# Moving the final norm's weight multiplications of the early channels, and splitting the last scaling and its stores over two engines and two queues

## The chip, the cores and the metric

The kernel runs on one core of one Trainium2 chip. The metric is device microseconds (us) of one execution. A profiled execution comes with a trace in which time starts at the span's begin; TensorE is called PE there, the loading of its weights PEld, VectorE DVE, ScalarE ACT, GpSimd POOL and SyncE, which only issues DMAs here, SP.

## The reference

One layer of a decoder on 1024 tokens with 1024 channels, all float32. Only the end matters for this change:

```python
z = rms_norm(h, norm_ple_g[l])
gate = jax.nn.sigmoid(z @ w_ple_gate[l] + b_ple_gate[l])
h = h + gate * (p[l] @ w_ple_proj[l])
return rms_norm(h, norm_final_g)      # y = h * rsqrt(mean(h*h) + 1e-6) * norm_final_g
```

Ahead of it stand the input projection with a pooling mixer and a gated linear recurrence, the output projection, and a squared-ReLU MLP with 4096 hidden channels.

## The kernel before

All activations lie transposed, channels on the 128 partitions and tokens along the free dimension, until the last stage. The float32 products are made of float32r parts: a high and a low part of each operand, three matmuls for one (high by high, high by low, low by high). The MLP is multiplied by a scheme with seven block products in place of eight. TensorE is fed without a halt through most of the kernel.

The last stage is the gate (`ps_e`, from z and the gate weights), the projection of the per-layer input (`ps_j`), the residual sum and the final norm. The first 512 tokens are done with channels on partitions, for all eight channel blocks. For the other 512 tokens only channels 0 to 511, the *early* half, are done so. Their result is turned by DVE transposes within 32 by 32 blocks, a store to DRAM (`turn_out`, lines 1196 ff.) and a load (`turn_in`, line 1207), so that tokens come to lie on partitions. The *late* half, channels 512 to 1023, is computed with tokens on partitions from the start, in four blocks of 128 tokens, `i` = 0 to 3. `late[i]` is a tile of 128 tokens by 1024 channels; `quarter(i, 0)` is its early half of 512 channels, which comes from the turn, and `quarter(i, 1)` its late half.

For each block `i`:

- `gate_opened(i)`: the first of 24 gate matmuls, and DVE's addition of the bias to what it left in PSUM (line 1248). `gate_products` adds the other 23. The opening of block `i + 1` is put ahead of the last 12 products of block `i`, so the group that one sees in the trace is 24 matmuls, 11 of block `i`, 1 of `i + 1`, 12 of `i`.
- `token_proj(i)`: six matmuls of the projection (line 1263).
- `sigmoids(i)`: ACT's sigmoid of the gate (line 1278).
- `gated(i)`: DVE multiplies it by the projection (line 1283) and adds the late half of the residual (line 1285).
- `early_square(i)`: ACT squares the early half and sums it over its channels (line 1223), into `early_mean[i]`.
- `early_gain(i)`: DVE multiplies the early half by the final norm's weights (line 1227), and adds the constant EPS to `early_mean[i]` (line 1228).
- `mean(i)`: DVE squares and sums the late half on top of `early_mean[i]` (line 1217), into `means[i]`.
- `inverse(i)`: POOL raises it to the power -0.5 (line 1288).
- `scale_late(i)`: DVE multiplies the late half by that and by the norm's weights (line 1292).
- `scale_early(i)`: ACT multiplies the early half, which has its weights already, by it (line 1296).
- `leave_for(i)`: SP issues one store of 512 KB, for blocks 0 to 2 (line 1301).

The last block runs through `token_last` (from line 1303 on): sigmoid and gating in two cuts of 256 channels; the sum of squares of the first cut on ACT (line 1314) and of the second on DVE; the root on POOL; then the scaling of both halves, and two stores of 256 KB (line 1327).

The order of instructions on PE, DVE and ACT in this stage is the order in which the code issues them: `pin` keeps it. Only `inverse`, which is all that POOL does, and the last two stores stand outside it. `early(0)` does the squares and weight multiplications of blocks 0 and 1 while block 1 is at its gate, and `early(2)` those of blocks 2 and 3 right after the mean of block 1.

Of the kernel before, what the change touches and what calls it, by code (L numbers as in the profile page):

```python
# [40 lines left out]
NTOK = 4  # L41
NQUAD = 4 * P
# [21 lines left out]
def block_kernel(  # L64
# [17 lines left out]
    nc = tc.nc  # L82
# [23 lines left out]
    def leave(name):  # L106
        spaces.pop(name).close()
# [24 lines left out]
    def bank(name):  # L132
        return pd.tile([P, HALF], F32, tag="pd", name=name)
# [27 lines left out]
    def got(ps):  # L161
        if ps.shape[-1] > HALF:
            return ps.rearrange("p (b j a) -> p b a j", b=2, a=2)
        return ps.rearrange("p (j a) -> p a j", a=2)

    def by(x, ps):
        if ps.shape[-1] > HALF:
            return x.rearrange("p (b a j) -> p b a j", b=2, a=2)
        return x.rearrange("p (a j) -> p a j", a=2)
# [7 lines left out]
    def pin(ins):  # L177
        return tc.keep_in_program_order(ins) if in_order else ins
# [324 lines left out]
    for k in range(NT):  # L503
# [3 lines left out]
        for hs in halves:  # L507
            if k == hs.start == 0:
                whi, wlo = (t[:, :HALF] for t in weight_tiles("wl0"))
                g = col("g_mix", 0)  # L510
                x, zhi, zlo = (t[:, hs] for t in (H[0], *A[0]))
# [9 lines left out]
            x, zhi, zlo = (t[:, hs] for t in (H[k], *A[k]))  # L521
# [597 lines left out]
    early_mean, means, inverses = ([ms[:, 4 * x + i : 4 * x + i + 1] for i in range(NTOK)] for x in range(3))  # L1119
# [45 lines left out]
    token_out = out[:, NT * HALF :].rearrange("p (i x) -> p i x", i=NTOK)  # L1165
# [35 lines left out]
    def quarter(i, half):  # L1201
        return late[i][:, half * NQUAD : (half + 1) * NQUAD]
# [9 lines left out]
    def mean(i, cut=slice(0, NQUAD)):  # L1212

        n = cut.stop - cut.start
        x = quarter(i, 1).rearrange("p (g x) -> p g x", g=4)[:, :, cut.start // 4 : cut.stop // 4]
        pin(
            nc.vector.tensor_tensor_reduce(
                square[:, :n].rearrange("p (g x) -> p g x", g=4), x, x, 1.0 / D, early_mean[i], ALU.mult, ALU.add, means[i]
            )
        )  # L1220

    def early_square(i):
        pin(nc.scalar.activation(T[5][:, SECOND], quarter(i, 0), AF.Square, scale=D**-0.5, accum_out=early_mean[i]))

    def early_gain(i):
        x = quarter(i, 0)
        pin(nc.vector.tensor_tensor(x, x, g_row[:, :NQUAD], ALU.mult))
        pin(nc.vector.tensor_scalar_add(early_mean[i], early_mean[i], EPS))

    def token_slice(i):  # L1230
# [20 lines left out]
    def token_gate(i, pg):  # L1251
        gate_products(i, pg, range(1, 12))
        ahead = gate_opened(i + 1) if i < NTOK - 1 else None
        gate_products(i, pg, range(12, 3 * NT))
        return ahead

    def token_proj(i, pj, cut):
        ts = token_slice(i)
        for k, (hi, lo, wh, wl) in enumerate(ple):
            for n, (z, w) in enumerate(((hi, wh), (hi, wl), (lo, wh))):  # L1260
                w = w[:, NQUAD + cut.start : NQUAD + cut.stop]
                pin(
                    nc.tensor.matmul(
                        pj, z[:, ts], turns(w), start=k == n == 0, stop=k == len(ple) - 1 and n == 2
                    )
                )
# [7 lines left out]
    def sigmoids(i, pg, cut=slice(0, NQUAD)):  # L1274
        t = T[3 + i % 2][:, FIRST]
        whole = cut.stop - cut.start == NQUAD
        got_a, by_a = (got(pg), by(t, pg)) if whole else (got(pg)[:, cut.start // 256], t[:, cut])
        pin(nc.scalar.activation(by_a, got_a, AF.Sigmoid))

    def gated(i, pj, cut=slice(0, NQUAD)):  # L1280

        t, e = T[3 + i % 2][:, FIRST][:, cut], T[3 + i % 2][:, SECOND][:, cut]
        pin(nc.vector.tensor_tensor(by(e, pj), by(t, pj), got(pj), ALU.mult))
        y = quarter(i, 1).rearrange("p (g o x) -> p g o x", g=4, x=32)[:, :, cut.start // P : cut.stop // P]
        pin(nc.vector.tensor_tensor(y, y, e.rearrange("p (o g x) -> p g o x", g=4, x=32), ALU.add))

    def inverse(i):
        nc.gpsimd.tensor_tensor(inverses[i], means[i], power, ALU.pow)

    def scale_late(i, cut=slice(0, NQUAD)):  # L1290
        y = quarter(i, 1)[:, cut]
        pin(nc.vector.scalar_tensor_tensor(y, y, inverses[i], g_row[:, NQUAD:][:, cut], ALU.mult, ALU.mult))

    def scale_early(i, cut=slice(0, NQUAD)):
        x = quarter(i, 0)[:, cut]
        pin(nc.scalar.activation(x, x, AF.Identity, scale=inverses[i]))

    def leave_for(i, cut=slice(0, NQUAD)):
        to = token_out[:, i].rearrange("p (h x) -> p h x", h=2)
        tc.keep_in_program_order(  # L1300
            nc.sync.dma_start(to[:, :, cut], late[i].rearrange("p (h x) -> p h x", h=2)[:, :, cut])
        )

    def token_last(i, pg, pj):

        cuts = slice(0, 256), slice(256, NQUAD)
        for cut in cuts:
            sigmoids(i, pg, cut)
        scale_early(i - 1)
        leave_for(i - 1)  # L1310
        gated(i, pj[0], cuts[0])
        y = quarter(i, 1).rearrange("p (g x) -> p g x", g=4)[:, :, :64]
        pin(
            nc.scalar.activation(
                T[5][:, HALF : HALF + 256].rearrange("p (g x) -> p g x", g=4), y, AF.Square, scale=D**-0.5, accum_out=means[i - 1]
            )
        )
        gated(i, pj[1], cuts[1])
        pin(nc.vector.tensor_tensor(early_mean[i], early_mean[i], means[i - 1], ALU.add))
        mean(i, cuts[1])  # L1320
        inverse(i)
        scale_early(i, slice(0, 256))
        rest = quarter(i, 0)[:, 256:]
        pin(nc.vector.tensor_scalar_mul(rest, rest, inverses[i]))
        scale_late(i)
        for half in range(2):
            nc.sync.dma_start(token_out[:, i, half * NQUAD : (half + 1) * NQUAD], quarter(i, half))

    for g, hs in enumerate(GROUPS):
        if g == 1:  # L1330
# [2 lines left out]
        for n, o in enumerate(ORDER[g]):  # L1333
# [14 lines left out]
            if g == 0 and 1 <= n < 5:  # L1348
                raw = wp.tile([P, S], F32, tag="raw", name=f"wg0_{n + 3}_raw")
                nc.sync.dma_start(raw, w_gate[n + 3])  # L1350
                x = slice((n - 1) * P, n * P)
# [27 lines left out]
    def early(first):  # L1379

        for x in range(first, first + 2):
            early_square(x)
            early_gain(x)

    in_order[:] = [True]
    opened = gate_opened(0)
    for i in range(NTOK):
        end = i == NTOK - 1
        pg, pj = opened
        if end:  # L1390
            token_gate(i, pg)
            pj = [x[:, :256] for x in (pj, bank("ps_j_end"))]
            for a, x in enumerate(pj):
                token_proj(i, x, slice(256 * a, 256 * a + 256))
            token_last(i, pg, pj)
            continue
        token_proj(i, pj, slice(0, NQUAD))
        opened = token_gate(i, pg)
        if i == 1:
            early(0)  # L1400
            mean(0)
            inverse(0)
        sigmoids(i, pg)
        if i > 0:
            scale_late(i - 1)
            scale_early(i - 1)
            leave_for(i - 1)
        gated(i, pj)
        if i == 0:
            continue  # L1410
        mean(i)
        inverse(i)
        if i == 1:
            early(2)
        if i == 2:
            scale_late(i)
    in_order.clear()
    leave("late")
    leave("sums")
# [80 lines left out]
```

## Time and profile before

| what | value |
|---|---|
| median of 3 runs | 919.76 us (919.32 to 919.93) |
| the profiled execution | 919.68 us |
| its span | 917.9 us, 11247 instructions |
| granted TensorE clock, mean | 0.998 |
| PE busy | 907.8 us (99%) |
| DVE busy | 700.8 us (76%) |
| ACT busy | 466.3 us (51%) |
| POOL busy | 39.1 us (4%) |

The span runs from the first to the last instruction; what the execution takes beyond it lies around the program. A row of the order of time gives the start in us, the duration in us, the engine, the line, the operation, what is written and read, the count, and in brackets how long the engine had been idle and what ended that. Successive instructions of one engine can overlap a little, so the pitch from start to start is shorter than the duration. A row of waits gives who waited for whom, the sum in us, the number of waits and the longest. A row of a DMA line gives the us from issue to landing, least, median and most. "edge" holds the small columns of sums and roots, "t_h" scratch tiles, "late" the blocks of the last stage, "turn" the buffers in DRAM through which the early half is turned.

### The profile page before, as it was taken

How to read it: one execution, taken by the hardware profiler on the slowest of the kernel's cores; microseconds unless marked ns; L12 is line 12 of the kernel's file. 1: busy time of each engine (PE TensorE's matmuls, PEld its weight loads, DVE VectorE, ACT ScalarE, POOL GpSimd, SP SyncE). 2: the span in 40 equal slices, each digit the busy share in tenths (PEclk: the TensorE clock that was granted, in tenths of full speed). 3: DMA queues.
4: the chain of work that ended last, by engine and by line, in shares of the span. 5: the costliest groups of instructions: out<-in, count | busy, mean ns of one | idle time of the engine just before them, and what ended most of it. 6: DMA issues, size and time to landing. Idle time of an engine off the chain costs nothing.

```text
span 917.9 us, 11247 instructions
## 1 busy us (share of the span) xinstructions
PE 907.8 (99%) x4221; PEld 791.2 (86%) x4221; DVE 700.8 (76%) x872; ACT 466.3 (51%) x602; POOL 39.1 (4%) x62
## 2 busy tenths in 40 slices
PE   9999999999999999999999999999999999999996
PEld 7888888888888888888888888888888888888885
DVE  7999974668876567656756899899876679799665
ACT  6569892447554454445444654353343436555322
POOL 4300001000000000000000000000000000000001
PEclk9999999999999999999999999999999999999999
DMA  7211145214478667766864987466633341041363
GB/s 273 101 47 45 48 160 144 76 46 120 111 206 223 201 167 229 224 184 176 243 196 165 355 321 278 138 202 203 205 113 100 115 161 46 1 138 47 104 181 117
DMA packets 56871, 142.47 MB, mean 155 GB/s; under 512 B 4976, under 2 KB 9968, under 8 KB 56816
## 3 DMA queue, kind: packets, MB, share of 16 engines
q1 hardware_dynamic: 52992, 132.31, 43.5%
q0 software_dynamic: 2736, 8.91, 5.8%
q10 hardware_dynamic: 1088, 0.52, 0.3%
q8 instruction: 33, 0.54, 0.3%
q14 instruction: 22, 0.18, 0.1%
HBM read 106.08 MB, written 35.65 MB: 154 GB/s over the span
## 4 chain that ended last, share of the span: by engine, by line
PE 96%; DMA 1%; DVE 1%; issue 1%; SPq 0%; POOL 0%; ACT 0%; DVEq 0%; POOLq 0%; ACTq 0%
PE ps_P_d L363 32%; PE ps_b_u L363 12%; PE ps_i L363 9%; PE ps_o L363 9%; PE ps_d_u L363 8%; PE ps_a_u L363 8%; PE ps_e L363 8%; PE ps_l L363 3%; PE ps_P_u L363 3%; PE ps_l L557 1%; PE ps_j L363 1%; PE ps_g L626 1%; PE ps_l_second L363 1%; PE ps_p L363 1%; DMA turn<-late 0%
## 5 line engine op out<-in xcount | busy, mean ns | idle before, releaser
L363 PE MATMUL ps_P_d<-a,wd_P_hi 128*128 128x512 f32 x880 | 261.8, 379 | 0.0
L363 PEld LDWEIGHTS ps_P_d<-a,wd_P_hi 128*128 128x128 f32 x880 | 166.5, 189 | 23.5
L363 PE MATMUL ps_P_d<-a,wd_P_lo 128*128 128x512 f32 x440 | 166.9, 379 | 0.0
L363 PE MATMUL ps_b_u<-a,wu_P 128*128 128x512 f32 x504 | 113.6, 379 | 0.0
L363 PEld LDWEIGHTS ps_b_u<-a,wu_P 128*128 128x128 f32 x504 | 95.3, 189 | 13.4
L363 PEld LDWEIGHTS ps_P_d<-a,wd_P_lo 128*128 128x128 f32 x440 | 83.2, 189 | 11.7
L363 PE MATMUL ps_a_u<-y,wu_P 128*128 128x512 f32 x360 | 82.6, 379 | 0.0
L363 PEld LDWEIGHTS ps_a_u<-y,wu_P 128*128 128x128 f32 x360 | 68.1, 189 | 9.6
L807 DVE TENSOR_TENSOR t_h<-t_h,ps_P_d 128x512 f32<-128x512 f32 (+1 forms) x56 | 42.4, 758 | 37.0 <-PE ps_P_d L363 37.0
L186 DVE TENSOR_TENSOR a<-wd,a 128x1024 fp32r<-128x1024 f32 x56 | 67.0, 1218 | 0.9 <-ACT a L185 0.6
L363 PE MATMUL ps_i<-a,wi_hi 128*128 128x512 f32 x256 | 66.1, 381 | 0.0
L363 PE MATMUL ps_o<-y,wo_hi 128*128 128x512 f32 x256 | 65.7, 379 | 0.0
L185 ACT ACTIVATE a<-wd 128x1024 fp32r<-128x1024 f32 x56 | 57.9, 1049 | 7.0 <-PE ps_P_d L363 7.0
L363 PEld LDWEIGHTS ps_i<-a,wi_hi 128*128 128x128 f32 x256 | 48.1, 189 | 7.9 <-PE ps_g L626 0.3
L185 ACT ACTIVATE wd_P_hi<-wd 128x1024 fp32r<-128x1024 f32 x24 | 25.3, 1056 | 58.0 <-PE ps_P_d L363 57.9
L363 PEld LDWEIGHTS ps_o<-y,wo_hi 128*128 128x128 f32 x256 | 48.4, 189 | 6.8
L825 DVE SCALAR_TENSOR_TENSOR t_h<-t_h,rstd 128x2048 f32<-128x2048 f32 x16 | 36.6, 2291 | 19.3 <-ACT t_h L844 19.3
L186 DVE TENSOR_TENSOR wu_P<-wu_raw,wu_P 128x512 fp32r<-128x512 f32 x45 | 30.9, 687 | 24.1 <-ACT wu_P L185 23.9
L186 DVE TENSOR_TENSOR wu_P<-wu,wu_P 128x512 fp32r<-128x512 f32 x47 | 32.3, 687 | 21.7 <-ACT wu_P L185 21.6
L363 PE MATMUL ps_d_u<-y,wu_P 128*128 128x512 f32 x180 | 41.3, 379 | 0.0
L363 PE MATMUL ps_d_u<-a,wu_P 128*128 128x512 f32 x180 | 41.3, 379 | 0.0
L185 ACT ACTIVATE wu_P<-wu 128x512 fp32r<-128x512 f32 x47 | 29.4, 625 | 20.0 <-PE ps_b_u L363 14.0
(252 smaller groups left out, 1538.6 us busy)
## 6 DMA issues: line engine op xcount, KB each, us to landing
wd<-act SPq DMA_DIRECT2D x56, 512.0 KB, 5.4
act<-t_h SPq DMA_DIRECT2D x32, 512.0 KB, 6.1
wu<-in_w_up SPq DMA_DIRECT2D x16, 512.0 KB, 4.9
act<-wu SPq DMA_DIRECT2D x16, 512.0 KB, 6.0
wd<-in_w_down SPq DMA_DIRECT2D x16, 512.0 KB, 5.9
wu_raw<-in_w_up SPq DMA_DIRECT2D x15, 512.0 KB, 5.3
t_h<-in_xT SPq DMA_DIRECT2D x14, 512.0 KB, 4.6
wg_raw<-in_w_gate SPq DMA_DIRECT2D x10, 512.0 KB, 3.3
```

Source lines behind the costliest of these rows:

```text
L185: first = pin(nc.scalar.activation(hi, src, AF.Copy))
L186: lowest[:] = [pin((eng or nc.vector).tensor_tensor(lo, src, f32(hi), ALU.subtract)).ins]
L363: ins = nc.tensor.matmul(ps, w, turns(z[:, hs]), start=first and z is zhi and w is whi, stop=last and w is wlo, skip_group_check=more,)
L557: nc.tensor.matmul(ps, kblk(w, o), turns(z[:, hs]), start=k == n == 0, stop=False)
L626: nc.tensor.matmul(x, w[r, o * P : (o + 1) * P], turns(z[r, at : at + HALF]), start=n == 0, stop=n == 2)
L807: (eng or nc.vector).tensor_tensor(to, to if y is None else y, x, ALU.add)
L825: nc.vector.scalar_tensor_tensor(cc, cc, 0.0, twice(R), ALU.max, ALU.mult)
```

## The change

The weight multiplication is cut loose from the addition of EPS, which becomes a function of its own, `floor`. `early` now only squares. The multiplication of block 0 comes after the mean and the root of block 0, that of block 1 after the mean and the root of block 1, those of blocks 2 and 3 after the late scaling of block 2. The additions of EPS stand right ahead of the mean that needs them, that of block 3 after the multiplications of blocks 2 and 3. In the last block ACT scales the whole early half, where DVE had taken the second 256 of its 512 channels, and the two last stores are issued one by ACT and one by SP, where SP had issued both.

```diff
     def early_gain(i):
         x = quarter(i, 0)
         pin(nc.vector.tensor_tensor(x, x, g_row[:, :NQUAD], ALU.mult))
+
+    def floor(i):
         pin(nc.vector.tensor_scalar_add(early_mean[i], early_mean[i], EPS))
...
         mean(i, cuts[1])
         inverse(i)
-        scale_early(i, slice(0, 256))
-        rest = quarter(i, 0)[:, 256:]
-        pin(nc.vector.tensor_scalar_mul(rest, rest, inverses[i]))
+        scale_early(i)
         scale_late(i)
-        for half in range(2):
-            nc.sync.dma_start(token_out[:, i, half * NQUAD : (half + 1) * NQUAD], quarter(i, half))
+        for half, queue in enumerate((nc.scalar, nc.sync)):
+            queue.dma_start(token_out[:, i, half * NQUAD : (half + 1) * NQUAD], quarter(i, half))
...
         for x in range(first, first + 2):
             early_square(x)
-            early_gain(x)
...
         if i == 1:
             early(0)
+            floor(0)
             mean(0)
             inverse(0)
+            early_gain(0)
         sigmoids(i, pg)
         if i > 0:
             scale_late(i - 1)
...
         gated(i, pj)
         if i == 0:
             continue
+        floor(i)
         mean(i)
         inverse(i)
         if i == 1:
             early(2)
+            early_gain(1)
         if i == 2:
             scale_late(i)
+            for x in range(2, NTOK):
+                early_gain(x)
+            floor(i + 1)
```

## The prediction

> **What bounds the kernel now.** I read the page first, then the waits of the last 34 us, then every instruction from 890 us in order of time, and last the stores to the output by line.
>
> ```profile
> span 917.9 us, 11247 instructions
> PE 96%; DMA 1%; DVE 1%; issue 1%; SPq 0%; POOL 0%; ACT 0%; DVEq 0%; POOLq 0%; ACTq 0%
> PE ps_e L1239 <- DVE ps_e L1248: 1.1, 1, 1.1
> ```
>
> The first two rows are the page's: 96% of the chain that ended last is TensorE. So an edit off TensorE pays only where TensorE stands still or after its last product. The third row is from the waits after 884 us: TensorE stands still once, for 1.1 us, and it is DVE that it waits for: the addition of the bias (L1248) that opens the gate product of a token block. The order of time shows why that addition is late.
>
> ```profile
> 890.62 5.34 PE L1239 MATMUL ps_e<-a 128*128 128x512 f32 x24
> 893.42 0.70 DVE L1248 TENSOR_TENSOR ps_e<-ps_e,t_h 128x512 f32<-128x512 f32 x1 [1.84 <-PE ps_e L1239]
> 894.96 0.69 DVE L1227 TENSOR_TENSOR late<-late,t_h 128x512 f32<-128x512 f32 x1 [0.84 <-ACT t_h L1223]
> 895.80 1.46 PE L1263 MATMUL ps_j<-proj,proj 128*128 128x512 f32 x6
> 896.40 0.57 ACT L1278 ACTIVATE t_h<-ps_e 128x512 f32<-128x512 f32 x1
> 897.10 5.34 PE L1239 MATMUL ps_e<-a 128*128 128x512 f32 x24
> 897.20 0.74 DVE L1217 CUSTOM_DVE_ANT_0 t_h<-late,edge 128x512 f32<-128x512 f32 x1
> 898.64 0.75 DVE L1292 SCALAR_TENSOR_TENSOR late<-late,edge,t_h 128x512 f32<-128x512 f32 x1 [0.69 <-POOL edge L1288]
> 899.31 0.68 DVE L1283 TENSOR_TENSOR t_h<-t_h,ps_e 128x512 f32<-128x512 f32 x1
> 900.75 0.75 DVE L1217 CUSTOM_DVE_ANT_0 t_h<-late,edge 128x512 f32<-128x512 f32 x1
> 901.43 0.69 DVE L1227 TENSOR_TENSOR late<-late,t_h 128x512 f32<-128x512 f32 x1
> 901.59 0.94 POOL L1288 TENSOR_TENSOR edge<-edge,power 128x1 f32<-128x1 f32 x1 [2.98 <-DVE edge L1217]
> 902.10 0.68 DVE L1227 TENSOR_TENSOR late<-late,t_h 128x512 f32<-128x512 f32 x1
> 902.48 0.60 ACT L1278 ACTIVATE t_h<-ps_e 128x512 f32<-128x512 f32 x1 [1.75 <-PE ps_e L1239]
> 902.76 0.69 DVE L1248 TENSOR_TENSOR ps_e<-ps_e,t_h 128x512 f32<-128x512 f32 x1
> 902.97 0.71 ACT L1296 ACTIVATE late<-late,edge 128x512 f32<-128x512 f32 x1
> 903.51 5.23 PE L1239 MATMUL ps_e<-a 128*128 128x512 f32 x23 [1.06 <-DVE ps_e L1248]
> 904.02 0.68 DVE L1283 TENSOR_TENSOR t_h<-t_h,ps_j 128x512 f32<-128x512 f32 x1
> 906.88 0.75 DVE L1292 SCALAR_TENSOR_TENSOR late<-late,edge,t_h 128x512 f32<-128x512 f32 x1 [0.66 <-POOL edge L1288]
> 908.77 0.66 ACT L1278 ACTIVATE t_h<-ps_e 128x256 f32<-128x256 f32 x2 [5.09 <-PE ps_e L1239]
> 909.51 0.42 DVE L1283 TENSOR_TENSOR t_h<-t_h,ps_j 128x256 f32<-128x256 f32 x1 [1.88 <-ACT t_h L1278]
> ```
>
> L1227 is the multiplication by the norm's weights. Four of them run; the two at 901.43 and 902.10 belong to blocks 2 and 3 and stand right before the bias addition of block 3 at 902.76. That addition needs only the first product of its group, and on the earlier block it came 893.42 - 890.62 = 2.80 after the group's start; so here it could run from 897.10 + 2.80 = 899.90. It runs 2.86 us later, and TensorE, through with its group, waits until 903.51. Much later, before 909.51, DVE is idle for 1.88 us.
>
> The tail after the last product:
>
> ```profile
> 911.10 0.15 DVE L1319 TENSOR_TENSOR edge<-edge 128x1 f32<-128x1 f32 x1
> 911.29 0.48 DVE L1217 CUSTOM_DVE_ANT_1 t_h<-late,edge 128x256 f32<-128x256 f32 x1
> 911.86 0.55 POOL L1288 TENSOR_TENSOR edge<-edge,power 128x1 f32<-128x1 f32 x1 [5.01 <-DVE edge L1217]
> 912.44 0.51 ACT L1296 ACTIVATE late<-late,edge 128x256 f32<-128x256 f32 x1 [1.45 <-POOL edge L1288]
> 912.44 0.35 DVE L1324 TENSOR_SCALAR late<-late,edge 128x256 f32<-128x256 f32 x1 [0.66 <-POOL edge L1288]
> 912.71 0.75 DVE L1292 SCALAR_TENSOR_TENSOR late<-late,edge,t_h 128x512 f32<-128x512 f32 x1
> 912.98 0.84 SPq L1327 DMA_DIRECT2D out<-late  x2
> ```
>
> And the stores: of line 1327 (the last two, 256 KB each) and of line 1301 (512 KB each, one per earlier block), from issue to landing; then the core's last waits; then the instruction queue in the window from 915 us:
>
> ```profile
> DMA to landing us min/median/max: 2.1/2.7/3.3
> DMA to landing us min/median/max: 2.6/2.6/2.6
> L1492 SPq EVENT_SEMAPHORE  x4: 28/28/28, 916.8 to 917.0; - x4
> q14 instruction: 1, 0.01, 0.7%
> ```
>
> The two issues take 0.33 us each, so the second is issued at 912.98 + 0.84 - 0.33 = 913.49, just behind the DVE scaling (912.71 + 0.75 = 913.46). It lands 3.3 us later, at 916.8, where SP's wait ends; the close takes the remaining 1.1 us to 917.9. The first half took only 2.1 us, and a whole block of 512 KB 2.6. The second half's surplus coincides with one packet of instruction code that a DMA engine moved from 915 us on.
>
> **The sum is made against** the profiled execution: 919.68 us, of which 917.9 is span and 1.78 lies around it. It is 0.08 under the median of the runs, 919.76. A measurement of this kernel tells about 0.2% (1.84 us) from no change, so "faster" begins at 917.92.
>
> **Part 1: the multiplications move, and the addition of the constant is split off.** No instruction is added or removed; four multiplications (0.69 us each, 0.60 from start to start without the small addition behind it: 902.10 - 901.43 = 0.67, of which that is 0.07) and four small additions change places on DVE. The new order, walked through with the pitches of these rows:
>
> - Block 0, from 894.96, when ACT's square lets DVE go: the small addition, then the mean. The mean reads its result, and such a pair stands 911.29 - 911.10 = 0.19 apart: mean at 895.15 instead of 897.20. POOL starts 901.59 - 900.75 = 0.84 after a mean, takes 0.55, and DVE follows 0.03 later (911.86 + 0.55 to 912.44): the reciprocal root is there at 896.57. Beside it runs the multiplication of block 0, 901.43 - 900.75 = 0.68 after the mean's start, at 895.83 to 896.52, hidden under POOL's time.
> - Late scaling of block 0 at 896.57 (before: 898.64). Gating of block 1 at 896.57 + 0.67 = 897.24; its sigmoid ended at 896.40 + 0.57 = 896.97, in time. Mean of block 1 at 897.24 + 1.44 + 0.11 = 898.79 (1.44 from 899.31 to 900.75; 0.11 for the small addition in front, 0.07 to 0.12). Multiplication of block 1 at 899.47, through at 900.07.
> - Bias addition of block 3 at 900.07 instead of 902.76, over at 900.76. TensorE needs it after its group: 897.10 + 5.18 = 902.28 (5.18 is the pitch 890.62 to 895.80). The wait is gone with 1.5 us to spare.
>
> What TensorE gains: the last group starts at 902.28 instead of 903.51, 1.23. Measured at the sigmoid that waits for its end: a group of 24 without a halt reaches its sigmoid 902.48 - 897.10 = 5.38 after its start, one of 23 by one matmul (5.18 / 24 = 0.22) less, 5.16; so at 907.44 instead of 908.77. **Gain 1.33** (bounds 1.06, the recorded halt, to 1.33). I take 1.33, which stands at the reader of the result.
>
> What is late next: the multiplications of blocks 2 and 3 now lie behind block 2's late scaling, ahead of the gating of block 3. Gating of block 2 waits for its sigmoid, 902.48 + 0.60, so 903.11 (before 904.02, behind DVE's queue); mean at 903.11 + 1.44 + 0.06 = 904.61; POOL 905.45 to 906.00; late scaling 906.03; multiplications 906.70 and 907.30; last small addition 907.90; DVE free at 907.97. The gating of block 3 wants to start at 909.51 - 1.33 = 908.18. So they fit into what was idle, with 0.2 us of cover; if POOL takes 0.94 as at 901.59, DVE is free at 908.36 and the end comes 0.2 later. Cost 0, bounds 0 to 0.4. On ACT, the early scaling of block 2 needs its multiplication (over by 907.4) and comes only after the last sigmoids, 908.1. The stores of blocks 0 and 1 are issued up to 2 us earlier by SP, into queues with nothing urgent. Nothing else in the kernel changes order.
>
> **Part 2: the last scaling.** ACT takes the whole early half (0.71, row 902.97, in place of 0.51), DVE loses its quarter (0.35; 912.71 - 912.44 = 0.27 from start to start) and begins with the late half at once. With the root there at 912.44 - 1.33 = 911.11, ACT ends at 911.82, DVE at 911.86. **Gain 0.27** for the last half.
>
> **Part 3: the stores.** One on ACT's queue, one on SP's, both issued at about 911.88, against 913.49 for the later one before: 1.60 earlier, which is the two gains together. How long do they take? Nothing in this trace issues two such stores at once. The bounds: 2.6 (512 KB by one issue; no reason for less, since the bytes are the same) and 3.3 (the second half before). ACT's queue was used once, beside SP's, for transposed blocks:
>
> ```profile
> turn<-late SPq DMA_DIRECT2D x4, 128.0 KB, 3.5
> turn<-late ACTq DMA_DIRECT2D x4, 128.0 KB, 4.0
> L1196 ACTq DMA_DIRECT2D turn<-late x4: 401/743/1257, 885.9 to 888.2; - x4
> ```
>
> There ACT landed 0.5 later, and its shortest issue was 0.40 against 0.33. I take 2.8: the 2.6 of the same bytes, 0.1 for ACT's longer issue and 0.1 for two at once. It is nearest to that row, because both halves then stream together as one block does, and the packet of code came at 915 us, behind SP's first landing: two landings close together leave it little data to delay. Landing at 911.89 + 2.8 = 914.7 instead of 916.8. **Gain 0.5 more** (bounds 0.7 to 0, and a loss of 0.5 where ACT lands as late as with the transposed blocks).
>
> The Trainium skill, page "DMA: Bandwidth & Descriptors", section "Issuing engines are not separate DMA queues", says that transfers started by different engines run on the same 16 DMA engines and interleave, and that issuing from several saves only the sequencer's time. By that rule the second queue is worth no more than one issue, 0.33, and the halves should land together. The trace does not show such a pair; that SP was held by DVE and not by its own first issue (913.46 against 912.98 + 0.33) speaks for the rule.
>
> **Sum:** 1.33 + 0.27 + 0.5 = 2.1; 919.68 - 2.1 = 917.6.
>
> **The rivals.**
>
> *The pair lands as the second half did, 3.3 after its issue.* For it: it is the only row of a last store with another in flight, and code for the close must still be fetched. Against it: the first half took 2.1, three whole blocks 2.6. Then only the earlier start counts: 919.68 - 1.33 - 0.27 = 918.1; with ACT 0.5 later still, 918.6. That is within 0.2%. The page's rule above goes this way: a second queue brings no shorter transfer.
>
> *DVE is late at block 3.* The cover is 0.2 us; a slow POOL, or a longer pitch of the moved multiplications, puts them on the path: 917.8 to 918.2.
>
> *The wait stays.* If the bias addition is held by something else than the multiplications, for instance the root of block 0 that stands ahead of the scaling, TensorE still waits and parts 2 and 3 alone remain: 919.68 - 0.27 - 0 to 0.5 = 918.9 to 919.4. Against it: the chain in DVE's order has no other late wait, and 1.5 us to spare.
>
> *Slower, by ACT's queue.* The ACT half is the last landing. It decides from 2.1 + 2.8 = 4.9 us after its issue: then nothing is gained. The longest landing of the transposed blocks, both queues, was
>
> ```profile
> DMA to landing us min/median/max: 2.1/3.6/5.5
> ```
>
> With 5.5: 911.87 + 5.5 = 917.4, 0.6 behind the old end: 920.3. Slower by over 0.2% needs 6.9. Against it: that row is of eight transposing stores at once, whereas a plain store of the same 2 KB rows landed in 2.6 three times out of three.
>
> **How the numbers follow.** Forecast, own range 917.3 to 918.0: 0.50. Long landing, 918.0 to 918.6: 0.28. DVE late: 0.10. Wait stays: 0.07. ACT's queue: 0.05, most of it within 0.2% of before. "Faster" (below 917.92) is the forecast without its upper edge and part of the DVE case: 0.50. Slower 0.03, the same 0.47. Low end: 2.6 for the pair and 0.3 that I have not seen, 917.1; high end 918.9, which leaves the unremoved wait and the very late queue outside.
>
> **What would show it.** TensorE's last gate group with no wait on L1248 and starting near 902.3; two multiplications between 906.5 and 908.0 on DVE; the first scaled quarter's gating near 908.2 waiting for ACT or TensorE, not queued; both stores issued within 0.1 us near 911.9; SP's last wait ending near 914.7. Wrong if that wait ends past 915.5, if the gating of block 3 runs back to back behind a multiplication, or if TensorE halts elsewhere.

## The result, and the profile after

The changed kernel takes 918.2 us in the median (917.72 to 918.95, 20 runs) against 919.94 (919.32 to 920.97, 20 runs) before: 1.74 us less, ratio 0.9981 with a 95% interval of 0.9974 to 0.9988. The profiled execution took 918.18 us; its span is 916.0. The order of time of the last stage, in the lines that answer to those shown of before (in this fence and the next, lines from 1228 to 1319 have a number 2 higher than before):

```profile
895.27 0.15 DVE L1230 TENSOR_SCALAR edge<-edge 128x1 f32<-128x1 f32 x1 [0.94 <-ACT t_h L1223]
895.46 0.75 DVE L1217 CUSTOM_DVE_ANT_0 t_h<-late,edge 128x512 f32<-128x512 f32 x1
896.13 0.69 DVE L1227 TENSOR_TENSOR late<-late,t_h 128x512 f32<-128x512 f32 x1
897.29 0.75 DVE L1294 SCALAR_TENSOR_TENSOR late<-late,edge,t_h 128x512 f32<-128x512 f32 x1 [0.47 <-POOL edge L1290]
897.32 10.31 PE L1241 MATMUL ps_e<-a 128*128 128x512 f32 x47
900.14 0.69 DVE L1227 TENSOR_TENSOR late<-late,t_h 128x512 f32<-128x512 f32 x1
900.75 0.69 DVE L1250 TENSOR_TENSOR ps_e<-ps_e,t_h 128x512 f32<-128x512 f32 x1
906.26 0.75 DVE L1294 SCALAR_TENSOR_TENSOR late<-late,edge,t_h 128x512 f32<-128x512 f32 x1 [0.66 <-POOL edge L1290]
906.93 1.29 DVE L1227 TENSOR_TENSOR late<-late,t_h 128x512 f32<-128x512 f32 x2
907.66 0.66 ACT L1280 ACTIVATE t_h<-ps_e 128x256 f32<-128x256 f32 x2 [3.75 <-PE ps_e L1241]
908.14 0.15 DVE L1230 TENSOR_SCALAR edge<-edge 128x1 f32<-128x1 f32 x1
908.40 0.42 DVE L1285 TENSOR_TENSOR t_h<-t_h,ps_j 128x256 f32<-128x256 f32 x1
```

The gate products of blocks 2 and 3 now stand in one row of 47 matmuls without a halt (before: 24, a halt of 1.06, 23). The bias addition starts at 900.75, right behind the multiplication of block 1, and is over 1 us before TensorE needs it. The two multiplications of blocks 2 and 3 fill 906.93 to 908.2, and the gating of block 3 starts at 908.40, 0.74 after its sigmoid as before (909.51 - 908.77). This execution was 0.22 later than that of before by 890 us, so the sigmoid at 907.66 stands for a gain of 1.33 where the clock difference shows 1.11.

The tail, then the landings of the last two stores, SP's last wait, and SP's closing instructions:

```profile
911.34 0.72 ACT L1298 ACTIVATE late<-late,edge 128x512 f32<-128x512 f32 x1 [1.45 <-POOL edge L1290]
911.34 0.75 DVE L1294 SCALAR_TENSOR_TENSOR late<-late,edge,t_h 128x512 f32<-128x512 f32 x1 [0.66 <-POOL edge L1290]
912.09 0.40 ACTq L1327 DMA_DIRECT2D out<-late  x1
912.12 0.33 SPq L1327 DMA_DIRECT2D out<-late  x1
DMA to landing us min/median/max: 2.4/2.6/2.8
SPq L1498 <- DMA out<-late: 2.2, 1, 2.2
L1498 SPq EVENT_SEMAPHORE  x11: 17/28/28, 912.5 to 916.0; - x11
```

Issues, landing and close are where the prediction put them, counted from the sigmoid: the last landing comes 7.2 after it, forecast 914.7 - 907.44 = 7.3. What it did not have is in no row of the span: this execution takes 918.18 - 916.0 = 2.18 us around its span, that of before 1.78. Over all 20 runs the time around the span is 2.08 to 2.18, median 2.13; for the kernel before, in the 30 runs of the first comparison below, 1.73 to 1.85, median 1.78.

### The profile page after: what moved, and what is told of

Same layout as the page of the kernel before. It is cut to its first block, busy times and chain, and to the rows that moved or that the text cites. A ratio compares the mean times of both kernels' runs of the same rounds, so it can differ in the third digit from the quotient of the medians.

```text
span 916.0 us, 11244 instructions
## 1 busy us (share of the span) xinstructions
PE 908.1 (99%) x4221; PEld 791.0 (86%) x4221; DVE 700.9 (77%) x871; ACT 466.7 (51%) x602; POOL 39.8 (4%) x62
## 4 chain that ended last, share of the span: by engine, by line
PE 98%; issue 1%; DVE 0%; ACT 0%; POOLq 0%; POOL 0%
PE ps_P_d L363 32%; PE ps_b_u L363 12%; PE ps_i L363 9%; PE ps_o L363 9%; PE ps_a_u L363 8%; PE ps_d_u L363 8%; PE ps_e L363 8%; PE ps_l L363 3%; PE ps_P_u L363 3%; PE ps_e L1241 2%; PE ps_l L557 1%; PE ps_j L363 1%; PE ps_g L626 1%; PE ps_p L363 1%; PE ps_l_second L363 1%
```

## The experiments

Two measures are used. *Tail* is the time in the trace from the start of block 3's first sigmoid to the end of the last instruction; it is free of what happened earlier, and kernels with the same tail gave it within 0.02. *Around* is the time of a run less its span, as the median of the runs.

| kernel | us, median | around | tail | VectorE's instructions |
|---|---|---|---|---|
| before | 919.94 | 1.78 | 9.13 | 1218 |
| changed | 918.20 | 2.13 | 8.39 | 1213 |
| order_only | 917.63 | 1.80 | 8.06 | 1214 |
| tail_only | 919.47 | 1.79 | 8.61 | 1217 |
| both_on_sp | 918.40 | 2.13 | 8.27 | 1213 |
| one_store | 918.00 | 2.16 | 8.35 | 1213 |
| changed_plus_1 | 917.56 | 1.79 | 8.37 | 1214 |
| changed_plus_5 | 919.05 | 1.76 | 9.27 | 1218 |
| before_plus_20 | 918.64 | 1.78 | 8.05 | 1238 |
| two_moved | 917.87 | 1.77 | 8.07 | 1216 |
| order_two_queues | 917.28 | 1.81 | 8.12 | 1214 |

The last column counts all rows of VectorE in the trace, semaphore and drain instructions too. The four kernels from order_only to one_store ran on one chip, the next four from changed_plus_1 to two_moved on a second and order_two_queues on a third, beside the kernel before each time (919.88, 919.96 and 919.71 there). Across chips the ratios below are the fairer measure. Each tail is that of one trace.

### The parts one by one

**order_only**, the changed kernel with the old tail:

```diff
-        scale_early(i)
+        scale_early(i, slice(0, 256))
+        rest = quarter(i, 0)[:, 256:]
+        pin(nc.vector.tensor_scalar_mul(rest, rest, inverses[i]))
         scale_late(i)
-        for half, queue in enumerate((nc.scalar, nc.sync)):
-            queue.dma_start(...)
+        for half in range(2):
+            nc.sync.dma_start(...)
```

> The changed kernel with the last scaling and the last stores as they were before (ACT 256 channels, DVE 256, both stores on SP). Theory (the bias addition's wait is the larger part, and comes from the order alone): TensorE's last gate group runs with no wait on the bias addition, the sigmoid of block 3 about 1.3 us earlier than before, span 917.9 - 1.3 = 916.6 if the second store lands 3.3 us after its issue again, 916.1 if it lands in 2.3 to 2.8. Rival (the gain is the tail's, the order only moves work about): span within 0.4 of 917.9. On the time around the span (1.78 before, 2.08 to 2.18 in the runs of the changed kernel): if the store on ACT's queue costs it, 1.8 here; if the order does, 2.1.

917.63 us, ratio to before 0.9973 (0.9962 to 0.9983): in the median more than the whole change brings. Time around the span 1.80, so it is not the order that costs it. The landings of its two last stores:

```profile
912.33 0.84 SPq L1329 DMA_DIRECT2D out<-late  x2
DMA to landing us min/median/max: 2.1/2.1/2.2
```

The issues are as far apart as before, on the same queue, and the second store lands in 2.2, not 3.3.

**tail_only**, the kernel before with the new tail:

```diff
-        scale_early(i, slice(0, 256))
-        rest = quarter(i, 0)[:, 256:]
-        pin(nc.vector.tensor_scalar_mul(rest, rest, inverses[i]))
+        scale_early(i)
         scale_late(i)
-        for half in range(2):
-            nc.sync.dma_start(...)
+        for half, queue in enumerate((nc.scalar, nc.sync)):
+            queue.dma_start(...)
```

> The kernel before with only the last scaling (ACT all of the early half, DVE the late half at once) and the last stores (one on ACT, one on SP) changed. Theory: TensorE still waits about 1.06 us for the bias addition; both stores are issued 0.27 earlier than the later one before, near 913.2, and land in 2.8 instead of 3.3: span 917.9 - 0.27 - 0.5 = 917.1. Rival (two queues bring nothing but the earlier issue): 917.6. Time around the span: 2.1 if the store on ACT's queue costs it, 1.8 if not; with 2.1 the whole is worth about 0.4.

919.47 us, ratio 0.9993 (0.9984 to 1.0001), so not told from no change by time; around 1.79 although a store is on ACT's queue. The halt, the issues and the landings:

```profile
903.46 5.23 PE L1239 MATMUL ps_e<-a 128*128 128x512 f32 x23 [1.03 <-DVE ps_e L1248]
913.15 0.41 ACTq L1325 DMA_DIRECT2D out<-late  x1
913.18 0.33 SPq L1325 DMA_DIRECT2D out<-late  x1
DMA to landing us min/median/max: 2.5/2.6/2.8
```

TensorE's halt stays: it belongs to the order. The tail is 8.61, between order_only's 8.06 and before's 9.13; the span of this trace, 917.3, lies between theory and rival. About 0.2 of it is a gap in VectorE's closing instructions in this trace (0.47 from its last but one semaphore to its drain, 0.11 before).

**both_on_sp** and **one_store**, the changed kernel with other last stores:

```diff
-        for half, queue in enumerate((nc.scalar, nc.sync)):
+        for half, queue in enumerate((nc.sync, nc.sync)):
```

and, for one_store,

```diff
-        for half, queue in enumerate((nc.scalar, nc.sync)):
-            queue.dma_start(token_out[:, i, half * NQUAD : (half + 1) * NQUAD], quarter(i, half))
+        nc.sync.dma_start(token_out[:, i], late[i])
```

> The changed kernel with both last stores issued by SP, one after the other. Theory (the second store was late before because it was issued late and met a packet of code; the queue itself brings little): issues at 912.1 and 912.45, second landing 2.4 to 2.8 after its issue, span 916.0 to 916.4. Rival (a second store behind the first on one queue takes 3.3 whatever comes): landing 915.8, span 916.9. Time around the span: 1.8 if the store on ACT's queue costs 0.35 there, so that the whole comes out at about 918.0 or better; 2.1 if it does not.

> The changed kernel with the whole last block in one store of 512 KB on SP. Theory: issue at 912.1, landing 2.6 later as the three whole blocks before it, 914.7; span 915.8, 0.2 less than the changed kernel. If the store on ACT's queue costs 0.35 around the span, that goes too: 917.6 in all. Rival (two queues stream faster than one): span 916.2 or more.

918.40 and 918.00; both within noise of the changed kernel (ratios to before 0.9983 and 0.9980, against 0.9981). Neither brings the time around the span down: 2.13 and 2.16. So ACT's queue does not cost it. The landings, of both_on_sp and of one_store:

```profile
DMA to landing us min/median/max: 2.1/2.2/2.3
DMA to landing us min/median/max: 2.6/2.6/2.6
```

A second store behind a first on one queue lands in 2.3: the 3.3 was not the queue's. By the tail, 8.27 and 8.35 against 8.39, two queues bring nothing; one store gains 0.04 of it, not the 0.2 expected.

### The packet of code

After these four, the time around the span went with the length of VectorE's stream and with nothing else tried: 1213 instructions gave 2.13 to 2.16, 1214 and more 1.78 to 1.80. Code comes in packets of 8 KB on the instruction queue q14. In the kernel before, 10 of its 22 packets come while VectorE is within nine instructions, mostly within three, of number 62, 190, 318 and so on, 128 apart; the last such step is near 1214. In the kernel before that packet falls among the last store's data (915.4); in all kernels with 1214 to 1217 instructions it comes 0.3 to 1.4 us after the span's end, with 1213 instructions 1.6 after it. Three kernels move this packet and leave the order of all else as it is. The filler is a memset of an unused column of 128x1, put where VectorE is idle near 888 us:

```diff
         opened = token_gate(i, pg)
+        for _ in range(N if i == 0 else 0):      # N = 1, 5 on the changed kernel, 20 on before
+            pin(nc.vector.memset(spare, 0.0))
```

> The changed kernel with one more tiny instruction on VectorE (a memset of an unused column, while VectorE is idle near 888 us). So far the time around the span was 1.78 to 1.80 where VectorE's stream had 1214 instructions or more (before, order_only, tail_only) and 2.13 to 2.16 where it had 1213 (the changed kernel, both_on_sp, one_store). Theory (0.35 us outside the span hang on how far VectorE's stream reaches, since its last block of code is fetched as it passes a certain instruction): 1214 instructions, time around the span 1.80, span unchanged near 916.05, in all 917.85. Rival (the ACT or SP side, or the total order, sets it): time around the span 2.13, in all 918.2.

917.56 us (ratio 0.9974, 0.9964 to 0.9984), around 1.79, tail 8.37. One instruction of no use takes 0.35 off the time around the span, and nothing else changes.

> The changed kernel with five such instructions: 1218 on VectorE, as in the kernel before. Theory (the packet of code comes as VectorE passes that instruction, and whatever store is in flight then lands late): the packet falls inside the span, about 2 us after VectorE's last scaling, near 914; the stores land 0.3 to 1.0 later than 2.8; time around the span 1.78; span 916.3 to 917.0. Rival (the second store before landed late for another reason): landing 2.8, span 916.05.

919.05 us (0.9988, 0.9979 to 0.9997), around 1.76, tail 9.27. Here are the landings, and the instruction queue's packet in the window from 913.9 to 914.5:

```profile
DMA to landing us min/median/max: 3.4/3.5/3.6
q14 instruction: 1, 0.01, 3.2%
```

The packet is back among the stores' data, and both land 0.8 to 1.0 later than in the changed kernel. The packet itself took about 0.3 us (3.2% of 16 engines over 0.6 us); why it costs three times that is not shown.

> The kernel before with twenty such instructions, all in an idle stretch of VectorE: the same order and the same tail, only the packet of code comes earlier, near 907. Theory: TensorE's wait of 1.06 stays, the second of the last stores lands 2.2 after its issue instead of 3.3, span 918.1 - 1.1 = 917.0, in all 918.8, which would be 1.1 of the change's 1.7 without any part of the change. Rival (two stores on one queue are slow by themselves): landing 3.3, 919.9 in all.

918.64 us, ratio 0.9984 (0.9975 to 0.9993): 1.32 less than before on this chip, about three quarters of what the change brings, with none of its edits. The packet came even earlier than expected, at 901.5. Its halt and its last stores' landings:

```profile
902.91 5.23 PE L1240 MATMUL ps_e<-a 128*128 128x512 f32 x23 [0.84 <-DVE ps_e L1249]
DMA to landing us min/median/max: 2.1/2.1/2.2
```

TensorE still halts, 0.22 less than before; why less is not shown, and it makes up the part of the 1.32 that the tail does not. The second store lands in 2.2, as order_only's does, and the tail is 8.05 instead of 9.13. So the 3.3 us were the packet of code, 1.08 of tail.

### Two of the four, and the tail's own price

**two_moved**, the kernel before with only two multiplications moved (`floor` is split off as in the change):

```diff
             early_square(x)
-            early_gain(x)
+            if first == 0:
+                early_gain(x)
+                floor(x)
...
+        if i == 2:
+            floor(i)
         mean(i)
...
             scale_late(i)
+            for x in range(2, NTOK):
+                early_gain(x)
+            floor(i + 1)
```

> The kernel before with only the multiplications of blocks 2 and 3 moved behind block 2's late scaling; those of blocks 0 and 1 and the whole tail stay as before. Theory (TensorE waits because two multiplications stand right ahead of the bias addition): bias addition at 902.76 - 1.33 = 901.4, over before TensorE needs it at 902.3, no halt; the same 1.3 us at block 3's sigmoid as with all four moved, and the span of order_only, 915.8, as long as the packet of code falls outside the last stores. Rival (all four moves are needed): a halt of some tenths stays.

917.87 us (0.9977, 0.9968 to 0.9987). The gate products of blocks 2 and 3 stand in one row of 47 again, but it takes 10.52 us, where all four moves gave 10.31:

```profile
897.61 10.52 PE L1241 MATMUL ps_e<-a 128*128 128x512 f32 x47
902.15 0.69 DVE L1250 TENSOR_TENSOR ps_e<-ps_e,t_h 128x512 f32<-128x512 f32 x1
```

The bias addition is over at 902.84. TensorE needs it at 897.61 + 5.18 = 902.79, and its next matmul starts at 902.90, with 0.32 instead of 0.22 to the one behind it. So a wait of 0.2 us is left, too short to show as idle time in the row: the rival's halt of some tenths. The sigmoid of block 3 comes 908.17 - 897.61 = 10.56 after the row's start, against 10.34 with all four moves and 11.67 before. By its tail (8.07) it stands with order_only. Moving the multiplications of blocks 2 and 3 brings 1.1 of the 1.33; moving those of 0 and 1 brings the last 0.2 and the cover.

The last four ran on one chip, three of them kernels seen above.

> The kernel of order_only (order changed, early half scaled by ACT and DVE together, then the late half by DVE) with its two last stores on ACT's and SP's queues. From block 3's first sigmoid to the span's end it was 8.06 us with the old scaling and both stores on SP, 8.27 with the new scaling and both on SP, 8.39 with the new scaling and two queues. Theory (the end follows from when the first 256 KB start, since both halves share the DMA engines; the new scaling starts them 0.2 later, and ACT's queue takes 0.1 more): 8.1 to 8.2. Rival (the new scaling is not what costs, the pair of queues is): 8.3 or more. VectorE has 1214 instructions: time around the span 1.80.

```diff
-        for half in range(2):
-            nc.sync.dma_start(...)
+        for half, queue in enumerate((nc.scalar, nc.sync)):
+            queue.dma_start(...)
```

Against order_only's edit above, this puts the early half's store on ACT's queue. Its issues and landings:

```profile
912.01 0.39 ACTq L1329 DMA_DIRECT2D out<-late  x1
912.51 0.33 SPq L1329 DMA_DIRECT2D out<-late  x1
DMA to landing us min/median/max: 2.1/2.2/2.3
```

> The kernel of order_only once more, to be timed on one chip with the changed kernel. Theory (order alone is worth more than the whole change): 917.6, 0.6 under the changed kernel, of which 0.35 is around the span. Rival (the difference was the chip's): equal to the changed kernel within 0.2.

> The changed kernel with one tiny instruction more on VectorE, on the same chip. Theory: around the span 1.80 against 2.13, 0.35 under the changed kernel and 0.3 over order_again. Rival: equal to order_again, so that the new tail costs nothing.

> The changed kernel itself, beside the other three on one chip: 918.2, with 2.13 around the span and 8.39 from block 3's sigmoid to the span's end.

| kernel | us, median | ratio to before, 95% | around | tail |
|---|---|---|---|---|
| order_two_queues | 917.28 | 0.9972 (0.9961 to 0.9983) | 1.81 | 8.12 |
| order_again | 917.45 | 0.9974 (0.9964 to 0.9983) | 1.78 | 8.05 |
| plus_1_again | 917.78 | 0.9977 (0.9968 to 0.9986) | 1.78 | 8.38 |
| changed_again | 917.99 | 0.9983 (0.9974 to 0.9992) | 2.15 | 8.38 |

The medians stand in the order that tail and around give, but for the first two: order_two_queues has the longer tail and a median 0.17 lower. The intervals of neighbours overlap, so the time alone does not tell each from the next; the tail, which repeats within 0.02, does. The four tails make a square: the old scaling gives 8.06 with one queue and 8.12 with two, the new scaling 8.27 and 8.38. Scaling costs 0.21 to 0.26, the second queue 0.06 to 0.11. In the tail both are losses; the whole time does not show the queue's. The two kernels with the old scaling and 1214 instructions are clear of the kernel before, and by tail and around together (0.6 to 0.7) and in the median (0.5 to 0.7) ahead of the changed one.

## Why the prediction was right, and where it was not

The time fell within the range, but 0.6 over the forecast's 917.6, outside the forecast's own 917.3 to 918.0 and beyond 917.92, where "faster" began. Of the 0.6, 0.35 is the time around the span, and 0.26 is the base: the sum started from 919.68, and the kernel before took 919.94 beside the changed one. That parts 2 and 3 come out right as a pair, 0.77 forecast and 0.74 in the tail, is luck: two errors offset each other. In its own terms:

- *Part 1, gain 1.33: right.* The halt is gone with the order alone and stays with the tail alone; bias addition, scaling and multiplications came in the predicted order. The root of block 0 was 0.4 late, since POOL took 0.95 there and not 0.55, which the spare time absorbed. The gating of block 3 was not delayed; the cover was 0.2 as reckoned. Two of the four moves alone bring 1.1 of it. One premise of this part was wrong and matters below: "No instruction is added or removed" holds for the arithmetic, but the new order alone took four semaphore rows from VectorE's stream (1218 before, 1214 in order_only).
- *Part 2, gain 0.27: wrong, a loss of 0.21.* The sum went by the later store's issue. But before, the first 256 KB had been under way for half a microsecond when the second was issued; where no packet of code meets it, the second then lands in 2.2. What counts is when the first bytes start: from the first issue to the last landing it took 2.6 to 2.8 in every kernel whose last stores the packet missed, with one store or two, one queue or two, and 3.6 and 3.8 in the two that it met. That fits two stores which share the DMA engines. ACT and DVE together had the early half ready 0.5 us after the root; ACT alone takes 0.72. The last issue moved forward and the first one back, by about 0.2, and the end follows the first.
- *Part 3, gain 0.5: wrong in its cause.* The 3.3 of the second store was no property of two stores on one queue. The packet of code was seen in the profile and was taken for a reason why 2.8 was likely, but not priced as a term of its own: 1.08 of tail. It left the stores because VectorE's stream became shorter by five instructions, not because of the queues: with five fillers it was back, and with four fewer (order_only) or one fewer (tail_only) than before it was already gone. Nor did two landings close together leave it little to delay: in changed_plus_5 it came at 914.0, not at 915, and delayed both. The landing of 2.8 itself was forecast right. The second queue itself costs 0.1.
- *Nothing around the span: wrong by 0.35.* The sum carried the 1.78 over unchanged. With 1213 instructions it is 2.13.

Worked out from the measured terms: 1.33 (halt) + 1.08 (packet) - 0.32 (scaling 0.21 and queue 0.11) - 0.35 (around) = 1.74, as measured. So near an agreement is partly chance: for the changed kernel with one filler the same terms give 2.09, and its medians were 2.40 and, repeated, 1.93 below before. The forecast had 1.33 + 0.27 + 0.5 = 2.1. The rival in which the pair lands late again, 918.1, comes nearest to the time, and that of a late DVE reaches 918.2, but neither is what happened: the landing was 2.8, and DVE was in time. In the rival of ACT's queue, "slower" would have needed 4.9 + 1.84 = 6.7, not 6.9; nothing hangs on it.

The Trainium skill, page "DMA: Bandwidth & Descriptors", section "Issuing engines are not separate DMA queues", was quoted for the second queue, and the runs bear it out: 8.27 and 8.38, or 8.06 and 8.12, are no gain. Applied to the kernel before as well, its sharing of the 16 engines would have put the end of the pair, by estimate, 2.6 after the first issue, as for one block of the same bytes: near 915.6, and not 916.8. That would have been a sign that something else held the second store.

## What to carry to other kernels

When the end is two stores whose landings overlap, count from the issue of the first bytes to the last landing; here a balanced split of the work that delayed the first store lost. Before a landing that is a microsecond longer than its fellows is credited to a queue, look for a packet of instruction code in its window, and try a filler instruction: if that moves it, the gain belongs to the place of the code and can be had, or lost, with an edit that has nothing to do with the store. And for effects below 0.2%, compare a stretch of the trace that begins at a common event, and watch the time around the span.

## What the runs showed of the hardware

One VectorE instruction more or less, a memset of 0.06 us off the path, moved the time around the span by 0.35 us (changed against changed_plus_1: 2.13 and 1.79 around; again 2.15 and 1.78 on another chip), and five of them moved the tail by 0.9 (8.39 to 9.27). One 8 KB packet of code on the instruction queue made a 256 KB store land 3.3 us after its issue instead of 2.2 (before against before_plus_20). The Trainium skill, page "Runtime: NRT & Kernel Launch", section "Instruction fetch mechanics", says that an engine's sequencer fetches its next block of code by its own DMA queue in blocks of 16 KiB and that this is mostly hidden. The trace has code on queues that carry nothing else, q8 and q14, but not a queue for VectorE alone: 10 of q14's 22 packets go with VectorE's count. These are of 8 KB, where the page has 16 KiB. And at the end of this kernel the fetch is not hidden: 1.08 us of tail. That the 0.35 us around the span are VectorE waiting for that code fits the counts and the times of the packets; what VectorE does after the span is in no row, so this stays an inference, as does the cause of the 0.2 us gap in tail_only.
